# A decoder layer's boundary between mixer and feed-forward: x kept on chip, a norm weight loaded later, sums taken before their scale

## The chip, the cores and the metric

The kernel runs as one program on one core of a Trainium2 chip. A core has a tensor engine (PE, with its weight loads shown as PEld), a vector engine (DVE), a scalar engine (ACT), GpSimd (POOL) and SyncE (SP), which issues most of the transfers; SBUF is its working memory and PSUM holds the tensor engine's sums. The metric is the device time of one execution in microseconds, the median of three runs. Profiles come from one further execution.

## The reference, cut to what matters

One layer (DEPTH is 1) on x of 256 tokens by 2048 channels, all in float32. The change lies where the mixer ends and the feed-forward part begins:

```python
mixed = jnp.concatenate([attn, ssm], axis=-1) @ w_out[l]
x = x + rms_norm(mixed, ln_mix_post[l])
h = rms_norm(x, ln_ffn_pre[l])
u = causal_depthwise_conv(h @ w_ffn_up[l], ffn_conv_w[l], ffn_conv_b[l])
gate, up = jnp.split(u, [FFN_HIDDEN], axis=-1)
f = (jax.nn.gelu(gate, approximate=True) * up) @ w_ffn_down[l]
x = x + rms_norm(f, ln_ffn_post[l])
```

`rms_norm(x, w)` is x divided by the root of its mean square over the channels, times w. FFN_HIDDEN is 5632, so `w_ffn_up` has 11264 columns. The middle x is used twice: normalised, as the input of the up projection, and unchanged, as the residual of the last line.

## The kernel before

**Products.** Every float32 product is made of three or fewer reduced products: each operand is split in a high part and the rest (`whi`, `wlo` for weights; two planes of `hT`, `mT`, `h2`, `gT` for activations). Weights come as units of 128 x 1024. `Weights.rounded` loads a unit (SP's queue, 512 KB), casts it to the high part on ACT (L72) and subtracts on DVE to get the low part (L73). `raw` has four buffers, `whi` and `wlo` seven each from L727 on. `tick()` starts one unit more each time a unit has been used, and then runs what `defer(n, ...)` has put n ticks ahead; `issue_after(end[0])` places that behind the last matmul on PE.

**Order.** Engines run their queues in order. The order in a queue is set by a planner when the program is built: it takes what it reckons to be ready, earlier statements first. Only the block under `manual_schedule` (L826) has the order of PE, ACT and DVE as it is written.

**The boundary.** `mm` holds mixed times the post norm's weight (`wpost`) for two groups of 128 tokens (t = 0, 1) in four chunks of 512 channels. Its rms factor `rs[t]` is known only when chunk 3 is done (`factor`). The up projection's input is made without the second norm's factor: `ml = mm * lnrow`, `xt = xt * lnrow` (`weighted`, `x_weighted`; `lnrow` is the second norm's weight), then `ml = ml * rs + xt` (`scaled`), four transposes on PE into PSUM (`turned`), a cast on ACT for the high and a subtraction on DVE for the low half of `h2` (`finish`). Since `x_weighted` has overwritten x, x is loaded again (L880, 1 MB for each t), and `second_rms` (L780) forms `x1 = mm * rs + x` in eight pieces (L784, the residuals), squares and sums each on ACT and takes the reciprocal root: the second norm's factor for each token. `along_tokens` (L175) turns it from a column into a row copied to all partitions, `rb2`, by two PE transposes.

**The up tiles.** A tile of 128 up columns for 256 tokens is 16 pairs of matmuls (L202 with 512 columns, L203 with 256) into one PSUM buffer; four buffers (`acc`) are used in rotation. Hidden tile i needs two, a gate and an up tile. The first three up tiles (`held_up`) are computed within the hand-ordered block, 128 tokens at a time. `cols_sum` (L216) adds the two halves of the PSUM buffer into SBUF (a copy on ACT, L218, and an add on DVE, L219), which frees the buffer; `conv_ffn` does this and then multiplies by `rb2`, applies the three taps of the convolution, and `gated` (L948) makes gelu(gate) times up and splits it into `gT`. 22 hidden tiles make a half; then come the down products of that half, and after the second half the last norm with its weight `wpo`.

The program's own statement of how the first up tiles are ended, which the change rewrites:

```python
        if half == 0:
            along_tokens(rb2, [sums[:, t:t + 1] for t in range(NT)])
        for i in range(half * HALF, (half + 1) * HALF):
            begun = held_up[2 * i:2 * i + 2]
```

Of the kernel before, what the change touches and what calls it, by code (L numbers as in the profile page):

```python
# [9 lines left out]
F32 = mybir.dt.float32  # L10
# [105 lines left out]
def decoder_layer(ctx, tc, x, xT, win, wdt, wout, wup, wdown, relb, vec, cols, mconv, fconv,  # L116
# [202 lines left out]
    with ExitStack() as mctx:  # L319
# [414 lines left out]
        ml = px.tile([P, NT, D], F32, name="ml")  # L734
# [4 lines left out]
        def weighted(t, c):  # L739

            nc.vector.tensor_tensor(ml[:, t, chunk(c)], mm[:, t, chunk(c)], lnrow[:, chunk(c)],
                                    op=ALU.mult)

        def x_weighted(t, c):
            nc.vector.tensor_tensor(xt[:, t, chunk(c)], xt[:, t, chunk(c)], lnrow[:, chunk(c)],
                                    op=ALU.mult)

        def post(c):
            def fn(t, ps):
                square_sum(ss[0][t][:, c:c + 1], ps)  # L750
                nc.vector.tensor_tensor(mm[:, t, chunk(c)], ps, wpost[:, chunk(c)], op=ALU.mult)
                weighted(t, c)
            return fn
# [7 lines left out]
        def scaled(t, q):  # L761

            h = ml[:, t, chunk(q)]
            nc.vector.scalar_tensor_tensor(h, h, rs[t], xt[:, t, chunk(q)], op0=ALU.mult,
                                           op1=ALU.add)

        def turned(t, q):

            pt = psum("pxt").rearrange("p (j c) -> p j c", c=P)
            for j in range(4):  # L770
                nc.tensor.transpose(pt[:, j, :], ml[:, t, q * 512 + j * P:q * 512 + j * P + P],
                                    ident)
            dst = [h2[:, q * 4:q * 4 + 4, c, tok(t)] for c in range(2)]
            last = [nc.scalar.copy(dst[0], pt).ins]

            def rest():
                last.append(nc.vector.tensor_tensor(dst[1], pt, f32(dst[0]), op=ALU.subtract).ins)
            return rest, last

        def second_rms():  # L780
            for t in range(NT):
                for q in range(4):
                    x1 = xt[:, t, chunk(q)]
                    nc.vector.scalar_tensor_tensor(x1, mm[:, t, chunk(q)], rs[t], x1, op0=ALU.mult,  # L784
                                                   op1=ALU.add)
                    square_sum(ss1[:, t, q:q + 1], x1)
# [4 lines left out]
        for t in range(NT):  # L791
            for c in range(4):
                defer(2 + t * 4 + c, x_weighted, t, c)
# [32 lines left out]
        with tc.manual_schedule(engines={E.PE, E.Activation, E.DVE}):  # L826
# [5 lines left out]
            weighted(0, 3)  # L832
# [10 lines left out]
            scaled(0, 3)  # L843
            t1_units(3, 4)
# [17 lines left out]
            more[0]()  # L862
# [4 lines left out]
            more[1]()  # L867
# [11 lines left out]
        for t in range(NT):  # L879
            aux(out=xt[:, t, :], in_=x[0, tok(t), :])  # L880
# [11 lines left out]
    aux(out=wpo, in_=row_bcast(V_FFNPOST, D))  # L892
    defer(12, nc.scalar.mul, wpo, wpo, -0.5)
# [4 lines left out]
    def conv_ffn(f, ps):  # L898
        wv = fcv[:, f, :]
        u, c = (fp.tile([P, S], F32, name="cf" + n, tag="cf", bufs=8) for n in "uc")  # L900
        cols_sum(u, ps)
# [46 lines left out]
    def gated(i, pg, pu):  # L948
        cg = conv_ffn(i, pg)
        nc.scalar.activation(cg, cg, AF.Gelu_apprx_tanh)  # L950
        cu = conv_ffn(NF + i, pu)
# [4 lines left out]
    held = []  # L956
    for half in range(2):
        if half == 0:
            along_tokens(rb2, [sums[:, t:t + 1] for t in range(NT)])
        for i in range(half * HALF, (half + 1) * HALF):  # L960
            begun = held_up[2 * i:2 * i + 2]
            pg, pu = begun + [col_psum() for _ in range(2 - len(begun))]
            for ps in (pg, pu)[len(begun):]:
                cols_tile(ps, h2)
            gated(i, pg, pu)
# [121 lines left out]
```

## Time and profile before

| what | value |
| --- | --- |
| median of three runs | 1148.11 us (1147.29 to 1148.58) |
| the profiled execution, its own time | 1148.41 us |
| its span, first to last instruction | 1146.6 us |
| PE busy, share of the span | 99% |
| DVE, ACT, POOL busy | 69%, 52%, 1% |
| bytes moved by DMA | 217.62 MB, 190 GB/s in the mean |

Busy time of PE counts modelled ends of pipelined matmuls, so a busy PE is not PE at its peak. The granted clock is a share of full speed. What an engine waited for is put down to the semaphore that came last.

### The profile page before, as it was taken

The page shows a single profiled execution, that of the slowest core. Times are in us where ns is not written, and L with a number is a line of the kernel's source. Part 1 is how long each engine was busy: PE and PEld are TensorE (multiplying, and loading weights), DVE is VectorE, ACT ScalarE, POOL GpSimd, SP SyncE. Part 2 cuts the span into 40 slices and gives each one's busy share as a digit, 9 for nine tenths or more (in the row PEclk, how much of TensorE's full clock was granted, in tenths as well). Part 3 has the DMA queues.
Part 4 walks back from the last instruction along what each step waited for, and adds up shares of the span by engine and source line. Part 5 has one row for each costly group of instructions (what it writes and reads, how often), then busy time and mean ns, then how long its engine had stood idle before and what let it go on. Part 6 is the DMA issues. An engine that isn't in the chain of part 4 may idle for free.

```text
span 1146.6 us, 15787 instructions
## 1 busy us (share of the span) xinstructions
PE 1129.6 (99%) x5912; PEld 958.4 (84%) x5912; DVE 796.4 (69%) x1270; ACT 591.4 (52%) x913; POOL 13.1 (1%) x24
## 2 busy tenths in 40 slices
PE   9999999999999979999999999999999999999997
PEld 7877888888888968888888888888888888888886
DVE  6587886776667768878787744447778777875553
ACT  6555544645454466555555544335555555544441
POOL 0000000000000100000000000000000000000000
PEclk9999999999999989999999999999999999999999
DMA  8756444655587474555655665655555655565651
GB/s 293 293 162 201 145 151 140 185 172 166 185 323 231 147 270 153 188 186 191 189 184 185 186 198 184 191 193 186 184 188 193 189 183 187 184 193 190 185 164 74
DMA packets 60436, 217.62 MB, mean 190 GB/s; under 512 B 7151, under 2 KB 7832, under 8 KB 59208
## 3 DMA queue, kind: packets, MB, share of 16 engines
q1 hardware_dynamic: 58696, 207.69, 56.1%
q0 software_dynamic: 1376, 8.58, 1.9%
q8 instruction: 46, 0.75, 0.3%
q10 hardware_dynamic: 288, 0.35, 0.1%
q14 instruction: 30, 0.25, 0.1%
HBM read 214.49 MB, written 2.11 MB: 189 GB/s over the span
## 4 chain that ended last, share of the span: by engine, by line
PE 94%; DMA 2%; DVE 2%; ACT 1%; issue 1%; POOL 0%; SPq 0%; POOLq 0%; ACTq 0%
PE pa L202 34%; PE pa L203 18%; PE pa L265 9%; PE pa L266 9%; PE pa L267 9%; PE ph L267 4%; PE ph L265 4%; PE ph L266 4%; DMA raw<-in_wup_dram 2%; PE pab L202 1%; DVE wlo L73 1%; PE pab L203 1%; PE py L568 1%; DMA raw<-in_win_dram 0%; ACT whi L72 0%
## 5 line engine op out<-in xcount | busy, mean ns | idle before, releaser
L73 DVE TENSOR_TENSOR wlo<-raw,whi 128x1024 fp32r<-128x1024 f32 (+1 forms) x385 | 469.4, 1221 | 270.2 <-ACT whi L72 269.4
L72 ACT CAST whi<-raw 128x1024 fp32r<-128x1024 f32 (+1 forms) x385 | 402.9, 1047 | 475.4 <-PE pa L202 222.8
L202 PE MATMUL pa<-h,whi 128*128 128x512 f32 x1360 | 482.4, 397 | 5.3 <-DVE cfu L219 5.3
L203 PE MATMUL pa<-h,wlo 128*128 128x256 f32 x1360 | 385.1, 283 | 0.0
L202 PEld LDWEIGHTS pa<-h,whi 128*128 128x128 f32 x1360 | 257.5, 189 | 66.7 <-ACT junk L185 3.8
L203 PEld LDWEIGHTS pa<-h,wlo 128*128 128x128 f32 x1360 | 257.6, 189 | 0.1
L202 PE MATMUL pa<-hT,whi 128*128 128x512 f32 x384 | 138.6, 399 | 0.0
L203 PE MATMUL pa<-hT,wlo 128*128 128x256 f32 x384 | 108.3, 283 | 0.2 <-DVE wlo L73 0.2
L905 DVE SCALAR_TENSOR_TENSOR cfc<-cfu,fcv,cfc 128x255 f32<-128x255 f32 (+1 forms) x176 | 84.5, 480 | 3.8 <-ACT cfc L903 1.0
L202 PEld LDWEIGHTS pa<-hT,whi 128*128 128x128 f32 x384 | 72.1, 188 | 16.6 <-issue 0.2
L203 PEld LDWEIGHTS pa<-hT,wlo 128*128 128x128 f32 x384 | 72.1, 188 | 0.9 <-DVE wlo L73 0.5
L267 PE MATMUL pa<-whi,gT 128*128 128x512 f32 x176 | 69.3, 394 | 0.0
L267 PE MATMUL ph<-whi,gT 128*128 128x512 f32 x176 | 69.3, 394 | 0.0
L265 PE MATMUL ph<-whi,gT 128*128 128x512 f32 x176 | 69.2, 393 | 0.0
L266 PE MATMUL ph<-wlo,gT 128*128 128x512 f32 x176 | 69.2, 393 | 0.0
L265 PE MATMUL pa<-whi,gT 128*128 128x512 f32 x176 | 69.1, 393 | 0.0
L266 PE MATMUL pa<-wlo,gT 128*128 128x512 f32 x176 | 69.1, 393 | 0.0
L903 ACT ACTIVATE cfc<-cfu,fcv 128x256 f32<-128x256 f32 x88 | 52.5, 597 | 0.4 <-DVE cfu L902 0.4
L265 PE MATMUL pa<-whi,hT 128*128 128x512 f32 x128 | 51.7, 404 | 0.2 <-DVE xsT L219 0.2
L267 PE MATMUL pa<-whi,hT 128*128 128x512 f32 x128 | 50.7, 396 | 0.0
L266 PE MATMUL pa<-wlo,hT 128*128 128x512 f32 x128 | 50.6, 395 | 0.0
L265 PE MATMUL pa<-whi,mT 128*128 128x512 f32 x128 | 50.5, 394 | 0.0
(231 smaller groups left out, 1149.2 us busy)
## 6 DMA issues: line engine op xcount, KB each, us to landing
raw<-in_wup_dram SPq DMA_DIRECT2D x176, 512.0 KB, 3.5
raw<-in_wdown_dram SPq DMA_DIRECT2D x88, 512.0 KB, 3.5
raw<-in_win_dram SPq DMA_DIRECT2D x87, 512.0 KB, 3.5
raw<-in_wout_dram SPq DMA_DIRECT2D x32, 512.0 KB, 3.7
xt<-in_x_dram POOLq DMA_DIRECT2D x4, 1024.0 KB, 6.6
xsq<-in_x_dram SPq DMA_DIRECT2D x2, 1024.0 KB, 7.2
xr<-in_xT_dram SPq DMA_DIRECT2D x7, 256.0 KB, 6.4
out_dram<-xt SPq DMA_DIRECT2D x6, 256.0 KB, 2.4
```

What stands on the lines that cost most here:

```text
L72: nc.scalar.copy(hi[:, s], raw[:, s])
L73: return lambda: nc.vector.tensor_tensor(lo[:, s], raw[:, s], f32(hi[:, s]), op=ALU.subtract)
L202: nc.tensor.matmul(ps, w[0][:, s], aT[:, k, :, :], start=(k == 0), stop=False)
L203: end[0] = nc.tensor.matmul(ps[:, :S], w[1][:, s], aT[:, k, 0, :], start=False, stop=(k == KT - 1)).ins
L265: nc.tensor.matmul(ps, a, w[0][:, s], start=(first and j == 0), stop=False)
L266: nc.tensor.matmul(ps, a, w[1][:, s], start=False, stop=False)
L267: end[0] = nc.tensor.matmul(ps, b, w[0][:, s], start=False, stop=(last and j == 1)).ins
L568: nc.tensor.matmul(py[:, i * 64:(i + 1) * 64], rows[:, t, g, i, :], xcs[t, g][:, i * 64:(i + 1) * 64], start=True, stop=True)
L903: nc.scalar.activation(c, u, AF.Identity, scale=wv[:, 2:3], bias=wv[:, 3:4])
L905: nc.vector.scalar_tensor_tensor(c[:, sh:], u[:, :S - sh], wv[:, 2 - sh:3 - sh], c[:, sh:], op0=ALU.mult, op1=ALU.add)
```

## The change

Four tiles of the boundary's pool take the place of `ml`, and products are put where the values are no longer needed: the second token group's scaled products in `wpost` and `lnrow`, a chunk of the first's in `mm`. `x_weighted` writes to these and leaves `xt` as it is, so that x isn't loaded again. Three of x's products move from `defer` into `post`. Chunk 3 of the first tokens forms x1 at once and multiplies that by `lnrow`. In the hand-ordered block the first waiting weight split comes earlier, and the later ones move up by one. `wpo` is loaded and scaled 60 ticks after the up tiles begin. `cols_sum` is taken out of `conv_ffn`: the sums of each hidden tile are taken as soon as its products are there, and for the first two hidden tiles `along_tokens` and `gated` are deferred to the fifth tick.

```diff
--- before.py
+++ after.py
@@ -731,25 +731,30 @@
         nc.scalar.mul(wpost, wpost, -0.5)
         lnrow = px.tile([P, D], F32, name="lnrow")
         aux(out=lnrow, in_=row_bcast(V_FFNPRE, D))
-        ml = px.tile([P, NT, D], F32, name="ml")
+
+        ml0, xl0 = (px.tile([P, 3, 512], F32, name=n) for n in ("ml0", "xl0"))
+        ml3, xl3 = (px.tile([P, 512], F32, name=n) for n in ("ml3", "xl3"))
+        ml = [[ml0[:, q, :] for q in range(3)] + [mm[:, 0, chunk(3)]],
+              [wpost[:, chunk(q)] for q in range(3)] + [ml3]]
+        xl = [[xl0[:, q, :] for q in range(3)], [lnrow[:, chunk(q)] for q in range(3)] + [xl3]]
         ss = [[pers.tile([P, 4], F32, name=f"ss{n}{t}") for t in range(NT)] for n in range(3)]
         ss1 = pers.tile([P, NT, 4], F32, name="ss1")
         h2 = pers.tile([P, KT, 2, S], F32R, name="h2", tag="h", bufs=1)
 
         def weighted(t, c):
 
-            nc.vector.tensor_tensor(ml[:, t, chunk(c)], mm[:, t, chunk(c)], lnrow[:, chunk(c)],
-                                    op=ALU.mult)
+            nc.vector.tensor_tensor(ml[t][c], mm[:, t, chunk(c)], lnrow[:, chunk(c)], op=ALU.mult)
 
         def x_weighted(t, c):
-            nc.vector.tensor_tensor(xt[:, t, chunk(c)], xt[:, t, chunk(c)], lnrow[:, chunk(c)],
-                                    op=ALU.mult)
+            nc.vector.tensor_tensor(xl[t][c], xt[:, t, chunk(c)], lnrow[:, chunk(c)], op=ALU.mult)
 
         def post(c):
             def fn(t, ps):
                 square_sum(ss[0][t][:, c:c + 1], ps)
                 nc.vector.tensor_tensor(mm[:, t, chunk(c)], ps, wpost[:, chunk(c)], op=ALU.mult)
                 weighted(t, c)
+                if t == NT - 1:
+                    x_weighted(t, c)
             return fn
 
         def factor(t, ps):
@@ -760,16 +765,24 @@
 
         def scaled(t, q):
 
-            h = ml[:, t, chunk(q)]
-            nc.vector.scalar_tensor_tensor(h, h, rs[t], xt[:, t, chunk(q)], op0=ALU.mult,
+            if (t, q) == (0, 3):
+                residual(t, q)
+                nc.vector.tensor_tensor(ml[t][q], xt[:, t, chunk(q)], lnrow[:, chunk(q)],
+                                        op=ALU.mult)
+            else:
+                nc.vector.scalar_tensor_tensor(ml[t][q], ml[t][q], rs[t], xl[t][q], op0=ALU.mult,
+                                               op1=ALU.add)
+
+        def residual(t, q):
+            x1 = xt[:, t, chunk(q)]
+            nc.vector.scalar_tensor_tensor(x1, mm[:, t, chunk(q)], rs[t], x1, op0=ALU.mult,
                                            op1=ALU.add)
 
         def turned(t, q):
 
             pt = psum("pxt").rearrange("p (j c) -> p j c", c=P)
             for j in range(4):
-                nc.tensor.transpose(pt[:, j, :], ml[:, t, q * 512 + j * P:q * 512 + j * P + P],
-                                    ident)
+                nc.tensor.transpose(pt[:, j, :], ml[t][q][:, tok(j)], ident)
             dst = [h2[:, q * 4:q * 4 + 4, c, tok(t)] for c in range(2)]
             last = [nc.scalar.copy(dst[0], pt).ins]
 
@@ -780,17 +793,16 @@
         def second_rms():
             for t in range(NT):
                 for q in range(4):
-                    x1 = xt[:, t, chunk(q)]
-                    nc.vector.scalar_tensor_tensor(x1, mm[:, t, chunk(q)], rs[t], x1, op0=ALU.mult,
-                                                   op1=ALU.add)
-                    square_sum(ss1[:, t, q:q + 1], x1)
+                    if (t, q) != (0, 3):
+                        residual(t, q)
+                    square_sum(ss1[:, t, q:q + 1], xt[:, t, chunk(q)])
             a = pers.tile([P, NT], F32, name="sum1")
             nc.vector.tensor_reduce(a, ss1, axis=AX.X, op=ALU.add)
             return mean_rsqrt(a, 1.0 / D)
 
-        for t in range(NT):
-            for c in range(4):
-                defer(2 + t * 4 + c, x_weighted, t, c)
+        for c in range(3):
+            defer(2 + c, x_weighted, 0, c)
+        defer(5, x_weighted, 1, 3)
         for c in range(2):
             rows_chunk(first[c], mT, hi, first=False, done=post(c))
         both = list(lo) + list(hi)
@@ -829,7 +841,6 @@
             rs.append(factor(0, pss[0]))
             scaled(0, 0)
             scaled(0, 1)
-            weighted(0, 3)
             scaled(0, 2)
             t1_units(0, 1)
             more = [ws.fetch_rounded()]
@@ -841,6 +852,7 @@
             finish(0, 0)
             finish(0, 1)
             scaled(0, 3)
+            more[0]()
             t1_units(3, 4)
             more.append(ws.fetch_rounded())
             t1_units(4, 5)
@@ -859,12 +871,11 @@
             first_tokens(2)
             turn(1, 1)
             finish(1, 0)
-            more[0]()
+            more[1]()
             finish(1, 1)
             first_tokens(3)
             scaled(1, 2)
             weighted(1, 3)
-            more[1]()
             second_tokens(0)
             turn(1, 2)
             scaled(1, 3)
@@ -876,8 +887,6 @@
             finish(1, 3)
             second_tokens(2)
             second_tokens(3)
-        for t in range(NT):
-            aux(out=xt[:, t, :], in_=x[0, tok(t), :])
         tick()
         came = rest[1, 3][1]
         with tc.issue_after(came[0]), tc.issue_after(came[1]):
@@ -889,16 +898,22 @@
     fcv = fp.tile([P, 2 * NF, 4], F32, name="fcv")
     aux(out=fcv, in_=fconv)
     wpo = fp.tile([P, D], F32, name="wpo")
-    aux(out=wpo, in_=row_bcast(V_FFNPOST, D))
-    defer(12, nc.scalar.mul, wpo, wpo, -0.5)
     gT = fp.tile([P, HALF, 2, S], F32R, name="gT")
     fa = pers.tile([P, NT, D], F32, name="fa", tag="mm", bufs=1)
     rb2 = pers.tile([P, S], F32, name="rb2", tag="rbc", bufs=1)
 
-    def conv_ffn(f, ps):
+    def load_post():
+        aux(out=wpo, in_=row_bcast(V_FFNPOST, D))
+        nc.scalar.mul(wpo, wpo, -0.5)
+
+    def summed(ps):
+        u = fp.tile([P, S], F32, name="cfu", tag="cf", bufs=8)
+        cols_sum(u, ps)
+        return u
+
+    def conv_ffn(f, u):
         wv = fcv[:, f, :]
-        u, c = (fp.tile([P, S], F32, name="cf" + n, tag="cf", bufs=8) for n in "uc")
-        cols_sum(u, ps)
+        c = fp.tile([P, S], F32, name="cfc", tag="cf", bufs=8)
         nc.vector.tensor_tensor(u, u, rb2, op=ALU.mult)
         nc.scalar.activation(c, u, AF.Identity, scale=wv[:, 2:3], bias=wv[:, 3:4])
         for sh in (1, 2):
@@ -945,24 +960,28 @@
                 nc.sync.dma_start(out=out[0, tok(t), q:e], in_=x1)
         return fn
 
-    def gated(i, pg, pu):
-        cg = conv_ffn(i, pg)
+    def gated(i, ug, uu):
+        cg = conv_ffn(i, ug)
         nc.scalar.activation(cg, cg, AF.Gelu_apprx_tanh)
-        cu = conv_ffn(NF + i, pu)
+        cu = conv_ffn(NF + i, uu)
         k = i % HALF
         nc.vector.tensor_tensor(cu, cg, cu, op=ALU.mult)
         split_evac(gT, k, slice(0, S), cu)
 
     held = []
+    defer(5, lambda: along_tokens(rb2, [sums[:, t:t + 1] for t in range(NT)]))
+    defer(60, load_post)
     for half in range(2):
-        if half == 0:
-            along_tokens(rb2, [sums[:, t:t + 1] for t in range(NT)])
         for i in range(half * HALF, (half + 1) * HALF):
-            begun = held_up[2 * i:2 * i + 2]
-            pg, pu = begun + [col_psum() for _ in range(2 - len(begun))]
-            for ps in (pg, pu)[len(begun):]:
-                cols_tile(ps, h2)
-            gated(i, pg, pu)
+            ps = held_up[2 * i:2 * i + 2]
+            for _ in range(2 - len(ps)):
+                ps.append(col_psum())
+                cols_tile(ps[-1], h2)
+            us = [summed(p) for p in ps]
+            if i < 2:
+                defer(5 - 2 * i, gated, i, *us)
+            else:
+                gated(i, *us)
         for c in range(4):
             if half == 0 and c >= 2:
                 held.append([psum("ph") for _ in range(NT)])
```

## Rows read from the trace of the kernel before

**Rows 1.** The page of the profiled execution: its span, the busy time of each engine with its share of the span and its instructions, and from the costliest groups the casts of the weights (line, engine, operation, tile; busy time and mean of one; idle time of the engine just before them and what ended most of it).

```profile
span 1146.6 us, 15787 instructions
...
PE 1129.6 (99%) x5912; PEld 958.4 (84%) x5912; DVE 796.4 (69%) x1270; ACT 591.4 (52%) x913; POOL 13.1 (1%) x24
...
L72 ACT CAST whi<-raw 128x1024 fp32r<-128x1024 f32 (+1 forms) x385 | 402.9, 1047 | 475.4 <-PE pa L202 222.8
```

**Rows 2.** Stretches of the boundary and one of the steady loop behind it, all instructions: from:to in us, its length, then busy time (and instructions) of PE, PEld, DVE, ACT and POOL, the granted clock of PE, the busy share of the DMA engines and GB/s.

```profile
402.35:413.61 11.26, 11.26 (x66) 9.72 (x64) 6.35 (x7) 7.52 (x11) 0.00 (x0) 1.00 0.87 320
413.61:417.28 3.67, 0.16 (x2) 0.03 (x1) 3.67 (x7) 3.67 (x7) 0.00 (x0) 1.00 0.60 214
417.28:420.43 3.15, 3.15 (x10) 2.30 (x10) 3.15 (x3) 3.12 (x8) 0.00 (x0) 0.57 0.30 77
420.43:423.59 3.16, 0.00 (x1) 0.00 (x0) 2.19 (x9) 1.85 (x4) 0.72 (x1) 0.88 0.98 345
423.59:435.03 11.44, 11.44 (x56) 9.74 (x56) 7.75 (x14) 7.43 (x12) 0.00 (x0) 0.85 0.63 205
435.03:436.87 1.84, 0.01 (x1) 0.03 (x1) 1.84 (x5) 1.31 (x3) 0.00 (x0) 1.00 0.29 20
436.87:441.62 4.75, 4.75 (x19) 4.09 (x19) 3.51 (x8) 1.78 (x4) 0.00 (x0) 0.64 0.65 216
...
470.00:492.50 22.50, 22.50 (x130) 19.66 (x129) 17.88 (x28) 12.74 (x21) 0.00 (x0) 1.00 0.58 188
```

**Rows 3.** PE's instructions in order of time behind 413 us: start, us, engine, line, operation; in brackets the idle time before it and what ended it.

```profile
417.28 0.47 PE L202 MATMUL pa<-h,whi 128*128 128x512 f32 x1 [3.51 <-DVE cfu L219]
...
418.31 0.63 PE L202 MATMUL pa<-h,whi 128*128 128x512 f32 x1
418.74 0.41 PE L203 MATMUL pa<-h,wlo 128*128 128x256 f32 x1
...
423.59 0.43 PE L179 MATMUL prb<-cst,rsr 128*128 128x128 f32 x2 [3.16 <-DVE rsr L148]
...
436.87 0.47 PE L202 MATMUL pa<-h,whi 128*128 128x512 f32 x1 [1.84 <-DVE cfu L219]
```

**Rows 4.** DVE's instructions in order of time, 398 to 444 us, with the same columns.

```profile
398.38 0.74 DVE L784 SCALAR_TENSOR_TENSOR xt<-mm,lsr,xt 128x512 f32<-128x512 f32 x1
...
403.58 1.23 DVE L73 TENSOR_TENSOR wlo<-raw,whi 128x1024 fp32r<-128x1024 f32 x1 [3.32 <-ACT whi L72]
...
407.92 0.75 DVE L784 SCALAR_TENSOR_TENSOR xt<-mm,lsr,xt 128x512 f32<-128x512 f32 x1
...
414.07 2.73 DVE L784 SCALAR_TENSOR_TENSOR xt<-mm,lsr,xt 128x512 f32<-128x512 f32 x4
416.72 0.42 DVE L219 TENSOR_TENSOR cfu<-pa,cfu 128x256 f32<-128x256 f32 x1
417.05 4.62 DVE L73 TENSOR_TENSOR wlo<-raw,whi 128x1024 fp32r<-128x1024 f32 x4
421.59 0.15 DVE L788 TENSOR_REDUCE sum<-ss 128x2 f32<-128x8 f32 x1
...
424.63 0.42 DVE L902 TENSOR_TENSOR cfu<-cfu,rb 128x256 f32<-128x256 f32 x1
...
443.22 0.42 DVE L191 TENSOR_TENSOR gT<-cfc,gT 128x256 fp32r<-128x256 f32 x1
```

**Rows 5.** The chain of work that ended last, 386 to 424 us: start, us, what.

```profile
394.68 7.74 DMA raw<-in_wup_dram
...
404.83 6.76 DMA raw<-in_wup_dram
...
412.80 0.71 ACT junk L185 x2
```

**Rows 6.** DMA issues by line with their size and the median time to landing, and then GpSimd's (POOL's) own instructions by time: the second reload of x and the load of the last norm weight.

```profile
raw<-in_wup_dram SPq DMA_DIRECT2D x176, 512.0 KB, 3.5
...
wpost<-in_vec_dram POOLq DMA_DIRECT2D x1, 1024.0 KB, 11.3
...
wpo<-in_vec_dram POOLq DMA_DIRECT2D x1, 1024.0 KB, 10.6
...
393.78 0.57 POOL L880 DMA_DIRECT2D xt<-in_x_dram  x1 [8.99 <-DVE ml L764]
...
397.99 0.53 POOL L892 DMA_DIRECT2D wpo<-in_vec_dram  x1
```

**Rows 7.** The instructions of the tile `wpost`: count, min/median/max ns, first and last start.

```profile
L730 POOL DMA_DIRECT2D wpost<-in_vec_dram x1: 531/531/531, 312.1 to 312.1; - x1
L731 ACT ACTIVATE wpost<-wpost x1: 1916/1916/1916, 329.7 to 329.7; 128x2048 f32<-128x2048 f32 x1
```

**Rows 8.** The hand-ordered block, DVE by time and then one row of PE: the fourth scaled piece of the first tokens, the start of the second half's scale, the first piece scaled with it, the low half that follows, and PE's products that take that low half.

```profile
381.78 0.74 DVE L764 SCALAR_TENSOR_TENSOR ml<-ml,lsr,xt 128x512 f32<-128x512 f32 x1
383.91 0.21 DVE L168 TENSOR_SCALAR lsa<-ss,esb 128x1 f32<-128x1 f32 x1 [1.39 <-ACT junk L185]
...
385.32 0.75 DVE L764 SCALAR_TENSOR_TENSOR ml<-ml,lsr,xt 128x512 f32<-128x512 f32 x1
385.99 0.68 DVE L777 TENSOR_TENSOR h<-pxt,h 128x512 fp32r<-128x512 f32 x1
...
386.97 1.18 PE L210 MATMUL pa<-h,whi 128*128 128x256 f32 x8
```

## The prediction

> **What bounds the kernel now.** I began with the page's busy shares [rows 1]: the tensor engine (PE) is busy for 99% of the span, so almost everything that is not PE work is hidden, and a change of this kind can only be worth what PE loses around the boundary it touches. The view by stretches shows that loss [rows 2]. From 402.35 us PE runs the first up tiles on the new activations. In its first stretch 64 matmuls (32 pairs of one 512-column and one 256-column product) take 11.26 us, 0.352 us a pair, and the steady stretch at 470 us has the same pace (130 matmuls, 65 pairs, in 22.50 us, 0.346, with the straddling ones counted). Between 413.61 and 441.62 us the pace breaks: three stretches hold nearly no PE work (3.67, 3.16 and 1.84 us), and behind each gap comes a stretch with a granted clock of 0.57, 0.85 and 0.64.
>
> PE's own instructions name what ended each gap [rows 3]. The first and third gap end with a vector-engine (DVE) add, L219, that sums an up tile out of PSUM; the second with the last step of the second norm's scale, L148, which the transposes of `along_tokens` wait for. Behind a gap a pair takes 0.64 us (418.31 to 418.95) in place of 0.352: that is the lower of the two clock levels, 1.2 for 2.4 GHz, and each time PE had just stood still.
>
> The whole loss: 73 pairs lie between 402.35 and 441.62 us (32, then 5 + 27, then 9, by the counts of rows 2). At 0.352 they need 25.7 us, and the two transposes 0.2 us. They took 39.27 us. So 13.4 us are lost, 8.7 of them as gaps and 4.7 as slow pairs.
>
> By PE's busy time alone only the 8.7 us of gaps could come back, and the profiled time could not fall below 1139.7 us. The Trainium skill (Perfetto Trace Analysis, Identifying the Most-Contended Engine) says that matmul busy share is no good measure of the distance to the roofline; the count of pairs agrees, since 4.7 us of loss are booked as busy here.
>
> Why the adds and the scale are late is read from DVE's order, which is a fixed queue [rows 4]. The first residual piece (L784) runs at 398.38, the second only at 407.92, the last four at 414.07; behind these comes the first PSUM sum (416.72), then four weight splits L73 (4.62 us), then the reduction at 421.59. Two things hold this queue. The weight splits wait: at 403.58 DVE had stood 3.32 us for a cast, whose DMA took 7.74 us where 3.5 is the median for that tile, and the next one on the chain 6.76 [rows 5, 6]. At the same time the second reload of x (1 MB, issued at 393.78) and the last norm weight (1 MB, 397.99) are in flight [rows 6], and the stretch at 402.35 moves 320 GB/s against 188 in the steady one [rows 2]. And the residuals need the reloaded x, since the boundary overwrites it with x times the norm weight.
>
> **The change, part by part.**
>
> *x stays on chip.* Two 1 MB loads and their waits go. DVE's products for the boundary are 15 in place of 16 (seven of x, seven of the norm output, one for chunk 3 of the first tokens), so 0.7 us less in a stretch where PE has no gap: worth nothing by itself. What it gives is that the residuals, whose scale is in use from 385.32 us [rows 8], no longer wait for a transfer after 398 us.
>
> *The last norm weight later.* 1 MB leaves the same 10 us. Its load now comes 60 half tiles after 402.35, at 2.81 us each: about 571 us, where the steady stretch moves 188 GB/s. It lands at worst 10.6 us later as now [rows 6]; its scaling on ACT is issued with it, and in ACT's queue it may stand ahead of casts. The like case is `wpost`: loaded at 312.1, scaled at 329.7 [rows 7], while the load landed after 11.3 us [rows 6], so the planner put that scaling well behind the landing. I take 0, with an upper bound of 5 us: ACT held for 10.6 us would use up two tiles' PSUM cover (11.2 us) and leave some six casts and copies, about 5 us, to catch up.
>
> *The order in the hand-written block.* One weight split (1.155 us by the four in 4.62 [rows 4]) and one product (0.67 by two starts, 385.32 and 385.99 [rows 8]) now stand before the second half's scale. DVE is free for 1.39 us there: scaled piece at 381.78, scale chain at 383.91. 381.78 + 2 x 0.67 + 1.155 = 384.3, so the chain starts 0.4 us later. The nearest consumer is the third piece's low half, done at 386.67, which PE takes at 386.97; that slack is 0.3 us. Cost 0 to 0.4, taken as 0.1. In return the freed raw buffer is refilled some 5 us earlier.
>
> *Sums before the scale.* The first two hidden tiles are now summed out of PSUM at once; their scaling, convolution and gating, and the transposes, come five half tiles later, a half tile being eight pairs, 2.81 us: 402.35 + 5 x 2.81 = 416.4 us. Is everything ready then? DVE's work between 397.8 and 416.4: one low half 0.6, seven residuals at 0.68 (2.73 for four), at most eight weight splits at 1.155, four sums at about 0.35: 0.6 + 4.8 + 9.2 + 1.4 = 16.0, done by 413.8; the scale chain behind takes 2.0 (421.59 to PE's start at 423.59), so 415.8. On ACT: eight squares at 0.71 [rows 5], eight casts of 1 and four copies come to 15 of 18.9 us. So the transposes find their input even if every other instruction goes first, and the PSUM sums, which need nothing but finished matmuls, come before 413.6. The first two gaps go, with their slow pairs. The cost is not below 0; above, 2 us if the queue idles that long.
>
> *What is late next.* From 417.2 DVE has two tiles' gating in one lump. One gating costs it, by the steady stretch, 17.88 us less eight splits (9.24) less four sums (1.67), halved: 3.5 us [rows 2, 4]. It is behind the splits, 1.155 in each 2.81 us, so 59% is left: 7.0 / 0.59 = 11.9, to 429.1; then the two sums of the third hidden tile, 0.7 / 0.59 = 1.2, to 430.3. PE needs that PSUM buffer (four in rotation, so the sixth tile from 402.35) at 402.35 + 5 x 5.63 + 0.2 = 430.7. The margin is 0.4 us. From above: before, the two gatings took from 424.63 to 443.64, 19.0 us [rows 4]; at that pace the sums are there at 436.9, a wait of 6.2, and one slow stretch as the last one (4.75 less 9 x 0.352 = 1.6), 7.8 us in all. I take 0.6, near the working from the steady stretch, since before's pace holds PE's own gaps and casts that waited for a halted PE.
>
> **Sum.** 13.4 back, less 0.1 and 0.6: 12.7 us. The profiled execution took 1148.41 us; less 12.7 is 1135.7. The median is 0.30 lower, so I predict 1135.4 us.
>
> **Rivals.**
> 1. *The lump holds the next PSUM sums.* By the upper bound above 13.4 - 0.1 - 7.8 = 5.5 us are gained: 1142.6. For it: DVE is 79% busy in the steady stretch (17.88 of 22.50), and the sums of the third tile are issued behind both gatings. Against: the planner fills in what is ready, and the low bound just fits. The Trainium skill (TensorE: Matmul & The Clock Gate, the table of the engine) has ScalarE and VectorE as strict first-in first-out queues; by that, a sum once queued behind the gatings cannot pass them, which is this rival. Rows 4 bear it out: the sum at 416.72 passed nothing.
> 2. *The first PSUM sum keeps its place in DVE's order* behind residuals and splits, so that the change does only half of what it says: the first gap and its slow pairs stay (3.67 + 5 x 0.29 = 5.1), the others go. 13.4 - 5.1 = 8.3: 1139.8. Against it: without the reload that order runs through some 5 us earlier.
> 3. *Slower: PE stops at the moved transposes.* They stand in PE's own order at 416.4 now and everything behind waits. If squares on ACT are queued behind casts that wait for PE to free a weight buffer, the scale comes late, and each 1 us costs 1 us and then slow pairs. It decides at a scale ready after 416.4 + 13.4 = 429.8; at 433 the time would be 1135 + 16.6 + 1.6 = 1153. For it: casts wait on PE all through the kernel (222.8 us in total on the up tiles' products alone) [rows 1]. Against: before, with the reload, the scale was ready at 423.55.
> 4. *No change*: PE's gaps move behind 442 us undiminished, 1148. Only DVE's total could do that, and it has 21% free.
>
> **How the numbers follow.** Forecast (a loss of up to 2 us left): 0.60. Rival 1: 0.17. Rival 2: 0.14. Rival 3: 0.05. Rival 4: 0.04. The forecast's own range is 1134.2 (all 13.4 back, and 0.5 for run to run) to 1137; taking in rivals 1 and 2 up to their prices gives 1134.2 to 1142.5, which leaves out about 0.15. A measurement tells about 0.2% (2.3 us) from no change; forecast and rivals 1 and 2 all pass it: faster 0.92, same 0.03, slower 0.05.
>
> **What would show it.** Right: no load of x after 383 us; casts between 397 and 412 with no DMA wait; the residuals done by about 406 and the four sums by 413; PE without a gap from 402 to 442 us and a granted clock of 1.00 throughout; the transposes at about 416 with no idle time before them. Rival 1 shows as a gap near 431 ended by a sum; rival 2 as one at 413.6; rival 3 as one at 416 ended by the scale. The forecast is wrong if any gap over 2 us is left before 450 us, or if PE shows a wait near 571 to 585 us, where the norm weight now lands.

## The result: half of the forecast's gain, and the profile after

The changed kernel takes 1141.78 us in the median of four runs (1141.75 to 1142.76); the kernel before, on the same chip, 1148.30 us (1147.29 to 1148.58). The ratio is 0.9947, 95% interval 0.9930 to 0.9964: 6.5 us faster. The forecast was 1135.4, so its sign was right, and the gain is half of the 12.7 us that were expected. The time lies outside the forecast's own range (1134.2 to 1137) and inside the wider one that takes in rivals 1 and 2.

From the page of the changed kernel, its span and the busy time of each engine, to be set against [rows 1]:

```profile
span 1140.0 us, 15818 instructions
...
PE 1126.8 (99%) x5912; PEld 957.3 (84%) x5912; DVE 788.4 (69%) x1268; ACT 592.2 (52%) x913; POOL 12.0 (1%) x22
```

PE is again busy for 99%, with 2.8 us less busy time than before: most of the slow pairs are gone. The profiled execution took 1141.79 us.

The boundary in stretches, with the columns of [rows 2] (from:to, length, busy time and instructions of PE, PEld, DVE, ACT and POOL, granted clock, DMA share, GB/s):

```profile
402.89:414.50 11.61, 11.61 (x69) 10.14 (x68) 8.57 (x12) 8.93 (x16) 0.00 (x0) 1.00 0.78 296
414.50:417.56 3.06, 2.97 (x18) 2.33 (x16) 2.65 (x4) 3.06 (x7) 0.00 (x0) 1.00 0.75 221
417.56:421.99 4.43, 0.00 (x1) 0.01 (x1) 3.26 (x9) 2.80 (x5) 0.72 (x1) 1.00 0.76 269
421.99:426.30 4.31, 4.31 (x17) 3.71 (x18) 4.31 (x10) 2.45 (x5) 0.00 (x0) 0.60 0.77 248
426.30:442.15 15.85, 15.85 (x92) 13.86 (x92) 13.70 (x28) 12.15 (x21) 0.00 (x0) 1.00 0.46 148
470.00:492.50 22.50, 22.50 (x129) 19.66 (x128) 17.54 (x29) 12.77 (x20) 0.00 (x0) 1.00 0.60 189
```

Three gaps have become one, 417.56 to 421.99 us, with one stretch at a clock of 0.60 behind it. All else runs at 1.00. PE's instructions in order of time show what ended the gap:

```profile
421.99 0.43 PE L179 MATMUL prb<-cst,rsr 128*128 128x128 f32 x2 [4.51 <-DVE rsr L148]
...
423.18 0.63 PE L202 MATMUL pa<-h,whi 128*128 128x512 f32 x1
423.60 0.41 PE L203 MATMUL pa<-h,wlo 128*128 128x256 f32 x1
423.82 0.63 PE L202 MATMUL pa<-h,whi 128*128 128x512 f32 x1
```

The first and the third gap of [rows 3], which L219 had ended, are gone; the middle one, which ends with the second norm's scale (L148), is still there, and at 4.51 us is longer than its 3.16 before. Behind it seven pairs, from 422.17 to 426.25, took 4.08 us in place of 7 x 0.352 = 2.46: 1.6 us more (a slow pair runs from 423.18 to 423.82). So 6.1 of the 13.4 us are still lost here, and PE began the up tiles at 402.89 where it had been 402.35: 0.5 more. 13.4 - 6.1 - 0.5 = 6.8, and the two profiled executions differ by 6.6.

Why the scale comes at 421.99 and not at 415.8 is read from POOL and ACT, in order of time (in brackets the idle time before, and what ended it):

```profile
397.99 0.58 POOL L899 DMA_DIRECT2D fcv<-in_fconv_dram  x1 [12.47 <-PE pxt L785]
398.56 0.54 POOL L906 DMA_DIRECT2D wpo<-in_vec_dram  x1
...
404.85 1.05 ACT L72 CAST whi<-raw 128x1024 fp32r<-128x1024 f32 x1 [3.08 <-DMA raw<-in_wup_dram]
...
406.89 1.92 ACT L907 ACTIVATE wpo<-wpo 128x2048 f32<-128x2048 f32 x1 [0.72 <-DMA wpo<-in_vec_dram]
...
417.65 0.64 ACT L185 ACTIVATE junk<-xt 128x512 f32<-128x512 f32 x1
```

The load of `wpo` did not move. POOL issues it at 398.56, where it was issued at 397.99 before [rows 6], with its scaling on ACT right behind its landing. The deferral places the statement 60 ticks on, but its order is tied to a matmul on PE alone; nothing in it holds POOL's queue, and the planner put the transfer where it had been before. And a cast waits 3.08 us for its weights. What happens on DVE, in order of time, with the columns of [rows 4]:

```profile
384.69 0.21 DVE L168 TENSOR_SCALAR lsa<-ss,esb 128x1 f32<-128x1 f32 x1
...
398.69 0.74 DVE L778 SCALAR_TENSOR_TENSOR xt<-mm,lsr,xt 128x512 f32<-128x512 f32 x1
...
405.93 1.23 DVE L73 TENSOR_TENSOR wlo<-raw,whi 128x1024 fp32r<-128x1024 f32 x1 [3.09 <-ACT whi L72]
407.07 2.73 DVE L778 SCALAR_TENSOR_TENSOR xt<-mm,lsr,xt 128x512 f32<-128x512 f32 x4
...
410.92 1.41 DVE L778 SCALAR_TENSOR_TENSOR xt<-mm,lsr,xt 128x512 f32<-128x512 f32 x2
412.25 0.75 DVE L219 TENSOR_TENSOR cfu<-pa,cfu 128x256 f32<-128x256 f32 x2
...
417.79 1.23 DVE L73 TENSOR_TENSOR wlo<-raw,whi 128x1024 fp32r<-128x1024 f32 x1 [0.34 <-ACT whi L72]
...
420.24 1.23 DVE L73 TENSOR_TENSOR wlo<-raw,whi 128x1024 fp32r<-128x1024 f32 x1
...
421.77 0.16 DVE L148 TENSOR_TENSOR rsr<-rsy,rsq 128x2 f32<-128x2 f32 x1
...
429.83 0.75 DVE L219 TENSOR_TENSOR cfu<-pa,cfu 128x256 f32<-128x256 f32 x2
```

One residual runs at 398.69. The next four stand behind a weight split that waits 3.09 us for that cast, and start at 407.07; the last two at 410.92. The last square on ACT begins at 417.65, and two more splits stand ahead of the scale's last steps (417.79 and 420.24). The sums, by contrast, are in time: 412.25, and for the third hidden tile 429.83.

The chain of work that ended last runs through the load and its scaling:

```profile
398.56 8.30 DMA wpo<-in_vec_dram
...
406.89 1.14 ACT wpo L907
```

### The profile page after: what moved, and what is told of

Its sections match the earlier page's. It is cut to its first block, busy times and chain, and to the rows that moved or that the text cites. A ratio compares the mean times of both kernels' runs of the same rounds, so it can differ in the third digit from the quotient of the medians.

```text
span 1140.0 us, 15818 instructions
## 1 busy us (share of the span) xinstructions
PE 1126.8 (99%) x5912; PEld 957.3 (84%) x5912; DVE 788.4 (69%) x1268; ACT 592.2 (52%) x913; POOL 12.0 (1%) x22
## 2 busy tenths in 40 slices
DMA packets 60148, 215.53 MB, mean 189 GB/s; under 512 B 7119, under 2 KB 7800, under 8 KB 59176
## 4 chain that ended last, share of the span: by engine, by line
PE 94%; DMA 2%; ACT 1%; DVE 1%; issue 1%; SPq 0%; POOL 0%; POOLq 0%; ACTq 0%
PE pa L202 35%; PE pa L203 18%; PE pa L265 8%; PE pa L266 8%; PE pa L267 8%; PE ph L267 4%; PE ph L266 4%; PE ph L265 4%; PE pab L202 1%; DMA raw<-in_wout_dram 1%; DMA wpo<-in_vec_dram 1%; DVE wlo L73 1%; PE py L568 1%; PE pab L203 1%; ACT whi L72 1%
## 5 line engine op out<-in xcount | busy, mean ns | idle before, releaser
L920 DVE SCALAR_TENSOR_TENSOR cfc<-cfu,fcv,cfc 128x254 f32<-128x254 f32 (+1 forms) x176 | 83.4, 479 | 1.9 <-ACT cfc L918 0.5
L266 PE MATMUL pa<-wlo,mT 128*128 128x512 f32 x128 | 50.2, 392 | 0.3 <-DVE wlo L73 0.3
```

Source lines behind the costliest of these rows:

```text
L266: nc.tensor.matmul(ps, a, w[1][:, s], start=False, stop=False)
L920: nc.vector.scalar_tensor_tensor(c[:, sh:], u[:, :S - sh], wv[:, 2 - sh:3 - sh], c[:, sh:], op0=ALU.mult, op1=ALU.add)
```

## The experiments

Two theories for the wait that is left. **A:** the 1 MB load of `wpo` and its scaling make the scale late: the transfer slows the weights, and the scaling holds ACT. **B:** the fixed order of DVE and ACT makes it late: residuals and squares are queued behind splits and casts which wait in turn, whatever they wait for. Where an edit is shown without a kernel's name, it is against the changed kernel.

**1. `wpo` really late.** Load and scaling get an order edge on the queue that they run in: behind the weights' load on SP at tick 60, behind their cast on ACT at tick 66 (`ws.load` and `ws.cast` are the load and the cast of the latest weight unit).

```diff
...
     def load_post():
-        aux(out=wpo, in_=row_bcast(V_FFNPOST, D))
-        nc.scalar.mul(wpo, wpo, -0.5)
+        with tc.issue_after(ws.load):
+            nc.sync.dma_start(out=wpo, in_=row_bcast(V_FFNPOST, D))
+
+    def scale_post():
+        with tc.issue_after(ws.cast):
+            nc.scalar.mul(wpo, wpo, -0.5)
...
     defer(60, load_post)
+    defer(66, scale_post)
```

> The last norm weight really loaded late: on SyncE's queue behind the weight load of the 60th half tile, and scaled six half tiles after that. Theory A (its 1 MB, in flight from 398.6 us, and its scaling, which holds ScalarE at 406.9 us, make the second norm's scale late): the cast that waited 3.1 us for its weights no longer waits, the scaling's 0.7 us of wait and 1.9 us are gone from ScalarE, the scale is ready 3 to 5 us earlier, and PE's wait at the moved transposes falls from 4.5 us to under 1.5, with fewer slow pairs behind it: 1136 to 1138.5 us. Theory B (the fixed order of VectorE and ScalarE, squares and residuals behind weight splits and casts, makes it late by itself): the scale moves by 1 us or less, 1140.5 to 1142 us.

Measured: 1138.34 us (1137.68 to 1139.31), ratio 0.9919 (0.9905 to 0.9934). The tile `wpo` (instructions with min/median/max ns, first and last start; the time to landing):

```profile
L907 SPq DMA_DIRECT2D wpo<-in_vec_dram x1: 373/373/373, 563.2 to 563.2; - x1
L911 ACT ACTIVATE wpo<-wpo x1: 1907/1907/1907, 589.5 to 589.5; 128x2048 f32<-128x2048 f32 x1
...
DMA to landing us min/median/max: 5.6/5.6/5.6
```

It is now loaded at 563.2. The cast that had waited 3.08 us, and PE at the transposes (ACT's and PE's instructions in order of time):

```profile
403.85 1.05 ACT L72 CAST whi<-raw 128x1024 fp32r<-128x1024 f32 x1 [1.80 <-DMA raw<-in_wup_dram]
...
419.76 0.43 PE L179 MATMUL prb<-cst,rsr 128*128 128x128 f32 x2 [2.12 <-DVE rsr L148]
...
420.85 0.40 PE L202 MATMUL pa<-h,whi 128*128 128x512 f32 x1
```

The cast waits 1.80, PE 2.12 us, and no pair behind it is slow. That is the time that A gave (1136 to 1138.5), so the transfer or its scaling is a cause. A's signs came only in part: the cast was to wait no longer, and PE less than 1.5 us. 2.1 us of wait remain with both gone, so they are not the only cause.

**2. Only the scaling late.** The load stays early, and the order on ACT and DVE is that of run 1.

```diff
...
-    def load_post():
-        aux(out=wpo, in_=row_bcast(V_FFNPOST, D))
-        nc.scalar.mul(wpo, wpo, -0.5)
+    aux(out=wpo, in_=row_bcast(V_FFNPOST, D))
+
+    def scale_post():
+        with tc.issue_after(ws.cast):
+            nc.scalar.mul(wpo, wpo, -0.5)
...
-    defer(60, load_post)
+    defer(66, scale_post)
```

> Only the scaling of the last norm weight is late; its 1 MB load stays where the change has it, at about 398.6 us. The orders of ScalarE and VectorE come out as in the run with both late, so the difference between the two is the transfer alone. Theory A by the transfer: the cast still waits 3 us for its weights, PE's wait falls by 2 us at most: 1139 to 1141 us. Theory A by ScalarE's hold: as good as both late, 1136 to 1138.5 us. Theory B: 1140.5 to 1142 us.

Measured: 1141.08 us (1140.28 to 1144.20), ratio 0.9947 (0.9928 to 0.9967): what the change itself gives. The same two places:

```profile
405.11 1.05 ACT L72 CAST whi<-raw 128x1024 fp32r<-128x1024 f32 x1 [3.75 <-DMA raw<-in_wup_dram]
...
407.65 1.06 ACT L72 CAST whi<-raw 128x1024 fp32r<-128x1024 f32 x1 [0.94 <-DMA raw<-in_wup_dram]
...
421.08 0.69 PE L179 MATMUL prb<-cst,rsr 128*128 128x128 f32 x2 [4.13 <-DVE rsr L148]
```

The cast waits 3.75 us, the next one 0.94, and PE 4.13. Against the changed kernel PE's wait is only 0.4 us shorter without ACT's 1.92 us of scaling: the casts wait longer for their weights, and the order on DVE differs too, so the scaling's own worth isn't shown to the tenth. Run 1 differs from this run by the transfer alone, and 4.13 - 2.12 = 2.0 us of PE's wait hang on it; no execution of run 1 was as slow as any of run 2. The time by itself (B had 1140.5 to 1142) would not have told A from B. How long the weights' loads take between 395 and 420 us, from issue to landing, in the changed kernel, in run 2 and in run 1:

```profile
DMA to landing us min/median/max: 3.4/4.5/7.4
```

```profile
DMA to landing us min/median/max: 3.4/4.4/7.6
```

```profile
DMA to landing us min/median/max: 3.5/4.4/5.7
```

The medians are within 0.1 us. It is the longest load that differs, 7.4 and 7.6 us beside the 1 MB transfer and 5.7 without it. The load that the waiting cast needs took 6.9 us in the changed kernel (issued at 397.9), 7.6 in run 2 (397.5) and 5.7 in run 1 (398.2), and DVE's queue stands behind that cast.

**3. The transposes two half tiles later.** The load of `wpo` stays early; the wait on PE is moved to where its input should be there.

```diff
-    defer(5, lambda: along_tokens(rb2, [sums[:, t:t + 1] for t in range(NT)]))
+    defer(7, lambda: along_tokens(rb2, [sums[:, t:t + 1] for t in range(NT)]))
...
-            if i < 2:
-                defer(5 - 2 * i, gated, i, *us)
+            if i < 3:
+                defer((7, 5, 1)[i], gated, i, *us)
```

> The change as it is, with the transposes and the first gatings at the seventh half tile in place of the fifth, and the third hidden tile's gating deferred with them. PE reaches the transposes 5.6 us later, so its wait of 4.5 us goes, whatever makes the scale late: 1135.5 to 1137 us by theories A and B. If the three gatings in one lump hold the next PSUM sums (the first rival of the prediction), a new gap of 2 to 5 us ended by a sum shows near 431 to 442 us: 1138 to 1142 us.

Measured: 1134.72 us (1134.41 to 1136.10), ratio 0.9889 (0.9875 to 0.9904). The stretches, with the columns of [rows 2]:

```profile
402.90:414.50 11.60, 11.60 (x68) 10.13 (x67) 9.61 (x14) 10.03 (x19) 0.00 (x0) 1.00 0.72 255
414.50:442.00 27.50, 27.50 (x159) 24.05 (x158) 25.96 (x53) 22.51 (x40) 0.72 (x1) 1.00 0.64 208
```

PE is busy throughout, at a clock of 1.00. The scale is nearly as late as in the changed kernel (421.0 us; here too the load is early); PE just has other work until then. So the rest of the loss was this one wait with the slow pairs behind it, and three gatings in one lump hold up no PSUM sum.

**4. The sums and the deferral alone.** The kernel before with only the last part of the change: x is loaded again, `wpo` is as before. Against the kernel before, the core:

```diff
...
+    defer(5, lambda: along_tokens(rb2, [sums[:, t:t + 1] for t in range(NT)]))
...
-        if half == 0:
-            along_tokens(rb2, [sums[:, t:t + 1] for t in range(NT)])
...
+            us = [summed(p) for p in ps]
+            if i < 2:
+                defer(5 - 2 * i, gated, i, *us)
```

> The kernel before with the sums and deferrals of the up tiles alone; x is still overwritten and loaded again, and the last norm weight is loaded and scaled as before. If the sums are what took away the first and third gap, both are gone here too, and PE waits at the moved transposes until the scale, ready at 423.5 us before: some 7 us and slow pairs, in all 8 to 9 lost of the 13.4 before: 1143 to 1144.5 us. If the reload of x was what mattered, little changes: 1146.5 to 1148.5 us.

Measured: 1142.56 us (1141.65 to 1143.78), ratio 0.9956 (0.9941 to 0.9971), a little better than expected. PE's waits:

```profile
415.94 0.47 PE L202 MATMUL pa<-h,whi 128*128 128x512 f32 x1 [2.56 <-ACT junk L185]
...
423.86 0.43 PE L179 MATMUL prb<-cst,rsr 128*128 128x128 f32 x2 [3.83 <-DVE rsr L148]
```

The first gap is a sum that is late after all, the second the scale. DVE ran that sum at 415.37, behind residuals that stood behind splits, which had waited for their casts (3.92 and 1.82 us); x itself had landed by 402.4. The row names ACT, which had been done. The third gap is gone.

**5. x kept on chip, alone.** The changed kernel without the sums and the deferral, and with `wpo` as before. Against the changed kernel, the core:

```diff
...
+            along_tokens(rb2, [sums[:, t:t + 1] for t in range(NT)])
...
-            us = [summed(p) for p in ps]
-            if i < 2:
-                defer(5 - 2 * i, gated, i, *us)
-            else:
-                gated(i, *us)
+            gated(i, pg, pu)
```

> The change without its sums: x stays on chip and the hand-ordered block is as changed, but the first tiles are scaled and gated in the old order and the last norm weight is loaded and scaled as before. If the parts add up, this gives what the sums alone did not (6.5 of the whole less 4.7 of the sums alone): 1145 to 1146.5 us, with the gaps of before still there, shorter by 1 to 2 us in all. If keeping x is worth more by itself (the residuals freed from the reload, as the prediction has it), 1141 to 1144 us.

Measured: 1142.66 us (1142.25 to 1143.47), ratio 0.9953 (0.9938 to 0.9968). The expectation was that the parts add up, and they don't: the sums alone give 4.7 us, x (with the reordered block that goes with it) 5.5, both together 6.5. The first sum on DVE, and PE's only wait:

```profile
412.16 0.42 DVE L219 TENSOR_TENSOR cfu<-pa,cfu 128x256 f32<-128x256 f32 x1
...
420.09 0.69 PE L179 MATMUL prb<-cst,rsr 128*128 128x128 f32 x2 [5.31 <-DVE rsr L148]
```

The first sum is in time without being moved in the program. What is left is again the scale, 5.31 us of it, since PE reaches the undeferred transposes sooner. The two parts overlap: run 5 has neither the first nor the third gap, run 4 no third and less of the first, and both leave the wait for the scale.

**6. The second norm's residuals stated first.** The order alone is changed; `wpo` is still loaded early.

```diff
+            sums = second_rms()
...
-            sums = second_rms()
```

(from behind the five ticks that follow the hand-ordered block to ahead of them)

> The change with the second norm's residuals and squares stated ahead of the five weight fetches in place of behind them, so that VectorE and ScalarE take them first; the last norm weight is still loaded at 398.6 us and scaled where the planner puts it. Theory B (the fixed order, residuals and squares behind splits and casts that wait): the scale is ready before PE comes to the transposes, its wait of 4.5 us is gone: 1134.5 to 1136.5 us. Theory A (the 1 MB in flight and ScalarE's hold): the transfer and the hold are still there, the scale comes 1 to 2 us earlier at most: 1139 to 1141 us.

Measured: 1136.41 us (1134.99 to 1136.79), ratio 0.9895 (0.9881 to 0.9910). DVE's residuals, the cast on ACT that waits longest, the end of the scale, and PE at the transposes:

```profile
398.38 4.72 DVE L778 SCALAR_TENSOR_TENSOR xt<-mm,lsr,xt 128x512 f32<-128x512 f32 x7
...
404.61 1.05 ACT L72 CAST whi<-raw 128x1024 fp32r<-128x1024 f32 x1 [2.79 <-DMA raw<-in_wup_dram]
...
417.49 0.15 DVE L148 TENSOR_TENSOR rsr<-rsy,rsq 128x2 f32<-128x2 f32 x1
...
417.69 0.43 PE L179 MATMUL prb<-cst,rsr 128*128 128x128 f32 x2 [0.87 <-DVE rsr L148]
```

All seven residuals are done by 403.1 and the scale at 417.6; PE waits 0.87 us for it. The casts still wait for their weights (one of them 2.79 us), but no residual stands behind that wait. So B holds as well: most of PE's wait goes with the order. Not all of it: the squares on ACT still stand behind that cast and behind the scaling of `wpo` (1.91 us at 408.82), and with load and scaling late (run 8) the scale comes 4.1 us earlier than here.

**7. Runs 1 and 3 together**, `wpo` really late and the transposes two half tiles later.

> The last norm weight late (as in the first run) and the transposes at the seventh half tile (as in the third). If both only remove the same wait, this is as fast as the third run, 1134 to 1135.5 us. If the 1 MB also costs PE something elsewhere, 1133 to 1134 us.

Measured: 1134.98 us (1134.52 to 1135.04), ratio 0.9885 (0.9869 to 0.9902), not to be told from run 3. Once PE doesn't stop at the transposes, the early transfer costs nothing that these runs can show.

**8. Runs 1 and 6 together**, `wpo` really late and the residuals first, with the transposes where the change has them.

> Residuals and squares stated first, and the last norm weight late. No wait is left at the transposes: 1134 to 1135.5 us. If the weight splits and casts, now some 5 us later on VectorE and ScalarE, come late for PE, a gap ended by a split shows between 403 and 415 us: 1135.5 to 1138 us.

Measured: 1134.85 us (1134.32 to 1135.96), ratio 0.9885 (0.9871 to 0.9900). Residuals, the scale and the third hidden tile's two sums on DVE, then the transposes on PE:

```profile
399.11 4.72 DVE L778 SCALAR_TENSOR_TENSOR xt<-mm,lsr,xt 128x512 f32<-128x512 f32 x7
...
413.37 0.15 DVE L148 TENSOR_TENSOR rsr<-rsy,rsq 128x2 f32<-128x2 f32 x1
...
427.91 0.42 DVE L219 TENSOR_TENSOR cfu<-pa,cfu 128x256 f32<-128x256 f32 x1
...
428.58 0.42 DVE L219 TENSOR_TENSOR cfu<-pa,cfu 128x256 f32<-128x256 f32 x1
...
417.39 0.38 PE L179 MATMUL prb<-cst,rsr 128*128 128x128 f32 x2
```

Here the forecast's picture is all there: residuals by 403.8, the scale at 413.5, the transposes at 417.39 with no idle time before them, and no wait of PE from 402 to 450 us.

**9. `wpo` really late in the kernel before.** x is loaded again; the edit is that of run 1.

> The kernel before, with x loaded again and the sums where they were, but the last norm weight's load and scaling really late (SP's queue at the 60th tick, the scaling at the 66th). Theory A (the transfer holds the weights that DVE's order waits for): the wait of the first cast after 400 us falls from 3.3 us to 2 or less, the residuals and the first PSUM sum come 1 to 3 us earlier, and the time is 1144 to 1147. Theory B (the order alone, with x's reload in front of it): the waits on PE stay as before within 0.5 us each, 1147.5 to 1148.8.

Measured: 1146.77 us in the median of ten runs (1144.14 to 1148.44), ratio 0.9992 (0.9983 to 1.0002): not told from no change. The cast that held DVE's queue, and PE's waits:

```profile
402.93 1.05 ACT L72 CAST whi<-raw 128x1024 fp32r<-128x1024 f32 x1 [4.68 <-DMA raw<-in_wup_dram]
...
414.27 0.47 PE L202 MATMUL pa<-h,whi 128*128 128x512 f32 x1 [0.71 <-ACT whi L72]
...
420.93 0.69 PE L179 MATMUL prb<-cst,rsr 128*128 128x128 f32 x2 [4.78 <-DVE rsr L148]
...
435.17 0.47 PE L202 MATMUL pa<-h,whi 128*128 128x512 f32 x1 [1.84 <-DVE cfu L219]
```

The time is within A's lines, but so near to no change that it decides nothing, and the mechanism is A's only in part. The cast waits 4.68 us and DVE 3.91 behind it, more than DVE's 3.32 before [rows 4]; x's own 1 MB (issued at 393.57, 9.1 us to landing) is in flight beside that weight's load until 402.7. The next casts no longer wait, and the first sum comes 3.0 us earlier (413.71 for 416.72), as A had it. PE's wait in front of the first tiles falls to 0.71 us, and the next one, at the transposes, grows to 4.78. So with x's load in place, taking `wpo` away shifts most of the loss from one gap to the next. Neither theory as I had put it covers this.

PE's wait for the scale, each from one profiled execution, with the median and its ratio to the kernel before on the same chip (the medians come from several chips, so the ratios compare better):

| kernel | PE's wait at the transposes, us | median, us | ratio |
| --- | --- | --- | --- |
| the change | 4.51 | 1141.78 | 0.9947 |
| 2: with the scaling on ACT late | 4.13 | 1141.08 | 0.9947 |
| 1: with the transfer late too | 2.12 | 1138.34 | 0.9919 |
| 6: transfer kept, residuals first | 0.87 | 1136.41 | 0.9895 |
| 8: residuals first, transfer and scaling late | 0 | 1134.85 | 0.9885 |
| 3: all kept, transposes later | 0 | 1134.72 | 0.9889 |

Both theories hold, in series: the transfer makes a weight late, and the order makes residuals and squares wait for that weight. By the ratios run 1 gains 3.2 us over the change, run 6 gains 6.0 and both together (run 8) 7.1, each known to about 2 us: they overlap. Runs 3, 7 and 8 beat both kernels and are the same within their intervals; 3 is the smallest edit.

## Why the prediction was right and wrong

The range held by luck: it reached up to 1142.5 us for the sake of rivals 1 and 2, and neither came. The gap of 4.51 us is over the 2 us that the prediction named as the sign of being wrong. The step that failed is the claim that the moved transposes find their input, and with it the load that was to come later and didn't.

**The loss, 13.4 us: right.** Runs 3, 7 and 8 leave no gap and no slow pair, and are 12.6, 13.1 and 13.3 us faster than the kernel before on the same chip. The count of pairs, which took in the 4.7 us that the busy share hides, is what gave this.

**x stays on chip: right that it helps, wrong in the reason.** No load of x after 383 us, and 2.1 MB less are moved (215.53 for 217.62). That the residuals would "no longer wait for a transfer" of x misread rows 4: before, the second reload, issued at 393.78, had landed after 8.5 us, at 402.3, and the trace shows no residual waiting for it. They stood behind splits whose weights came late, in loads of 7.7 to 11.1 us issued between 394 and 401 us beside the reload and `wpo`; in the changed kernel the loads of that stretch take 7.4 us at most. The place in the queue stayed.

**The last norm weight later: this step failed.** "Its load now comes 60 half tiles after 402.35": it came at 398.56. I took the deferral at its word, though its order edge is on PE and the load is on POOL. "That the change doesn't do what it says" was due as a rival for this part too, and I had weighed it only for the sums. By the ratios, a load that is really late (run 1) gains 3.2 us more. The price I gave it, 0, was right: in runs 1 and 7 PE has no wait between 555 and 620 us.

**The hand-ordered block: right.** The second half's scale chain starts at 384.69 where I had 384.3, but everything was already 0.39 later when PE reached this block; that much is spread between executions (in run 3, whose code is the same up to there, the first residual behind the block comes 0.8 us earlier than in the changed kernel). Of the 0.5 us that PE starts late, 0.15 are left to the block, where I had 0.1.

**Sums before the scale: the step that failed and carried the error.** The sums came as forecast, from 412.25 us on, so rival 2 is out. "So the transposes find their input even if every other instruction goes first" was wrong: I had added up the work of each engine, and left out the time in which it waits. ACT's 15 us were about right: it began at 397.46 and ended the last square at 418.38, which is 20.9 us, of which 3.08 and 0.72 were waits for transfers and 1.92 the scaling of `wpo`, 15.2 for the rest. That is 4.6 us behind the 413.8 that I had for DVE; the scale chain behind it took 3.6 us in place of 2.0, because one split stands ahead of it and one between its steps. Together 6.2 us: the scale is there at 421.99 and not at 415.8. The term "cost 0; above, 2 us if the queue idles that long" measured 4.5 us of gap and 1.6 of slow pairs. The place is rival 3's (PE stops at the moved transposes, with squares queued behind casts), but those casts waited for transfers and not for PE to free a buffer, and the size is far below the one from which that would have made the kernel slower. I had given it 0.05 and had priced only its far end.

**What is late next: right in kind, too dear.** The lump of two gatings held nothing: in run 8, with PE undelayed, the third tile's sums run at 427.91 and 428.58 (I had 430.3), and PE doesn't wait. The 0.6 us for it were 0, and rival 1 is out. The planner had queued the sums between the gatings' parts, so the fixed order on DVE did no harm there; the residuals behind the splits are where it did, as DVE's rows at 405.93 and 407.07 show. The Trainium skill (TensorE: Matmul & The Clock Gate, the table of the engine) has the vector engine's queue as strict first-in first-out, and these rows agree.

**The test I had named** would have caught it at once: "casts between 397 and 412 with no DMA wait" and "the residuals done by about 406" both failed, and the gap at the transposes was the sign written down for rival 3.

## What to carry to other kernels

A statement that is deferred is late only in the queues that it is ordered against: for each instruction that it issues, look for what holds it on its own queue, and in the trace for where it really ran. To say that an input is ready, add to an in-order engine's work the waits of whatever stands ahead in its queue; a transfer that nobody waits for can lengthen the one that everybody waits for. Where an engine must stop for a value, moving the stop behind more of its own work can be the smallest cure, as in run 3; parts that fill the same gap don't add up, so test them one by one against what is left.

## What the runs showed of the hardware

A 512 KB load that takes 3.5 us in the median [rows 6] took up to 7.6 us beside a 1 MB load (run 2) and 5.7 at most without it (run 1), by the loads whose landing the view gives. The medians in that stretch were the same, 4.4 us: the cost of a second transfer sat in the longest loads. With x's reload as well, in the kernel before, they took up to 11.1 us.

An idle time of PE did not always bring the lower clock level. Before, 1.84 us of idle time were followed by a stretch at 0.64 [rows 2, 3], that is, in part at 1.2 GHz; in run 1 a wait of 2.12 us (until 419.76), and in run 4 one of 2.56 us (until 415.94), were followed by pairs at full pace, with a granted clock of 1.00 for the next 4 us. What PE had done earlier differs between them; which part of that decides, these runs don't settle.
